# Up projections of a gated feed-forward layer: ten feature tiles by Strassen's seven products, where there were six such tiles

## The chip, the cores and the metric

The kernel runs on one core of a Trainium2 chip. The metric is the device time of one execution in microseconds. All times below come from one profiled execution or from repeated timed runs.

## The reference, cut to what matters

The kernel computes one encoder block: three token mixers, a gated merge with an output projection onto the residual, and a gated feed-forward layer with a convolution over tokens. The change lies in that last layer. S = 512 tokens, D = 1024, D_FF = 2816, all float32.

```python
def rms_norm(x, g):
    return x * lax.rsqrt(jnp.mean(x * x, axis=-1, keepdims=True) + EPS) * g

def conv_glu_ffn(h, w_up, w_conv, b_conv, w_down):
    a, u = jnp.split(h @ w_up, 2, axis=-1)          # w_up: 1024 x 5632
    return (jax.nn.gelu(dwconv3(a, w_conv, b_conv)) * u) @ w_down

x = x + merged @ w_out                               # the output projection
x = x + conv_glu_ffn(rms_norm(x, ffn_norm_g), w_up, w_conv, b_conv, w_down)
return rms_norm(x, final_norm_g)
```

## The kernel before, in words

Everything is held transposed, features on partitions and the 512 tokens along the free axis. Each float32 operand is split in a high half, rounded to the format that TensorE takes at full rate (fp32r), and a low half, the rest. A product is three matmuls, high x high, high x low and low x high (`mm3`, L370 to L372). A weight block comes from memory as a raw tile (`emit_raw`, L246; three raw buffers, `wr`), ScalarE rounds it (L336) and VectorE subtracts (L337); the split weights lie in a ring of four buffers (`w`). A planner, `weights`, emits these steps a fixed number of blocks ahead. Engines take their instructions in the order in which they stand in the program, so the order of emission is the order of each queue. `in_turn` keeps the chained steps of an engine in order; its helper's line is L270.

The output projection's loop (L1312 to L1323) makes eight feature tiles of x2, the new residual. Each is scaled and split (L376, L377) into HH and HL, and its squares are summed on POOL into `acc` (L1323). The row norm of x2 follows: the sum is transposed (L177), written to memory and read back (`td`, `U`), reduced (L202), scaled (L203), raised to -1/2 on POOL (L204), transposed (L205), written and read back broadcast as `rb` (L208, L210). The up projections do not wait for it: the norm's factor is applied to their result, in `conv` (L570: product with rb; L572 to L574: the three taps) and on POOL (L1453, then L270) after the gelu (L1451, with a table load on ScalarE). The product with the other projection is L1467 (VectorE).

The up projections run over 22 feature tiles f. A normal tile has two projections, `ua` and `uu`, of 8 blocks each: 16 products of 128 x 128 x 512. A tile in `SUP` takes both projections together as a 2 x 2 block product by Strassen's scheme with seven products instead of eight, on halves of 256 tokens (`up_seven`; products 1, 2, 4, 5, 7, 3, 6 in that order): in all 7 x 4 products of 128 x 128 x 256,. It needs differences of x's blocks (`x_forms(p)` for four pairs p of feature tiles: three differences on VectorE, L1341 to L1343; their rounding on ScalarE, L1345; two remainders on VectorE, L1346 and L1347) and sums of weight blocks. Product 1's weights are a difference made on VectorE (L1383). Four other products' sums are made by DMA: `up_load` loads one summand into a `ut` tile (SP), `up_sum` adds the other with an accumulating DMA (POOL). `up_weight` rounds and subtracts such weights (L1390 ScalarE, L1391 VectorE). A tile that is not in `SUP` is called a normal tile below: its 16 products of 512 columns are what 8 x 4 of 256 would be.

The down projection takes the first twelve feature tiles in seven products too (blocks "s") and the other ten plainly (blocks "k"), in an order `DOWN` with plain blocks between the others. Its sums are loaded late (L246 on a unit tile `u`, SP) with an accumulating DMA on POOL (L270). The residual x2 is transposed in tiles 3 to 10 (`turn_out`: L177 and four DMAs to memory) and loaded back (`turn_in`, L186) in tiles 6 to 13. The weights of a `SUP` tile come as one block `ub`.

Of the kernel before, what the change touches and what calls it, by code (L numbers as in the profile page):

```python
# [12 lines left out]
F32R = mybir.dt.float32r  # L13
# [4 lines left out]
P = 128  # L18
S = 512
# [6 lines left out]
NSP = 6  # L26
NOK = FT - 2 * NSP
HELD = 4
SUP = (5, 7, 9, 11, 13, 15)
UP_ORDER = (1, 2, 4, 5, 7, 3, 6)  # L30
HC = D // 2
NU = 14
# [105 lines left out]
def hybrid_block(ctx, tc, xT, memT, wflat, vecs, gbias, nabias, out):  # L138
# [121 lines left out]
        q = slice(j * HC, (j + 1) * HC)  # L260
        return lw[0][:, q], lw[1][:, q]

    ur, uf = [], {}

    chain = {}

# [1045 lines left out]
    for f in range(KT):  # L1312
        xr = scr()
        SY.dma_start(xr, xT[:, f, :])
        ps = proj(("out", f), GH, GL)
        V.tensor_tensor(x2[f], ps, xr, op=ALU.add)
        split_act(HH[f], HL[f], x2[f], vcol("ffn_g", f))
        if f == 0:
            A.activation(acc2, x2[f], AF.Square)
        else:  # L1320
            sq = scr()
            A.activation(sq, x2[f], AF.Square)
            G.tensor_tensor(acc2, acc2, sq, op=ALU.add)  # L1323


    x2v = [u[:, :4 * S].rearrange("p (f s) -> p f s", f=4) for u in x2u]
    ur.extend(unit() for _ in range(NSP // 2))
    ou, UH, UL = [], [], []
    res, turns = {}, {}
    xf = [unit(F32R) for _ in range(5)]  # L1330
    XF = (5, 2, 6, 7, 1)
    uw = {}

    def x_forms(p):

        y, d = ur[2][:, p % 2 * D:(p % 2 + 1) * D], ur[1][:, :5 * M]
# [8 lines left out]
        A.activation(h, d, AF.Copy)  # L1345
        V.tensor_tensor(xf[p][:, 5 * M:8 * M], d[:, :3 * M], h[:, :3 * M].bitcast(F32), op=ALU.subtract)  # L1346
        V.tensor_tensor(xf[4][:, p * S:(p + 1) * S], d[:, 3 * M:], h[:, 3 * M:].bitcast(F32), op=ALU.subtract)  # L1347

    def x_of(i, p):
# [27 lines left out]
    def up_weight(f, n):  # L1377
# [13 lines left out]
        V.tensor_tensor(l, src, h.bitcast(F32), op=ALU.subtract)  # L1391
        uw[f, "w", i] = h, l

    def up_seven(f):

        b12, b45, b7, b36 = [atps() for _ in range(4)]
        at = {1: b12[:, :M], 2: b12[:, M:], 4: b45[:, :M], 5: b45[:, M:], 7: b7[:, :M], 3: b36[:, :M], 6: b36[:, M:]}
        ta, tu = scr(), scr()
        t00, t01, t11 = ta[:, :M], tu[:, :M], tu[:, M:]
        for n, i in enumerate(UP_ORDER):  # L1400
            if n + 2 < len(UP_ORDER):
                up_weight(f, n + 2)
            elif n + 2 == len(UP_ORDER):
                emit_split(st["split"])
                st["split"] += 1
            wh, wl = uw.pop((f, "w", i))
            for p in range(KT // 2):
                c = slice(p * P, (p + 1) * P)
                xh, xl = x_of(i, p)
                mm3(at[i], wh[:, c], wl[:, c], xh, xl, p == 0, p == KT // 2 - 1)  # L1410
            if i == 2:
                A.activation(ta, b12, AF.Copy)
                A.activation(t11, at[2], AF.Copy, scale=-1.0)
                V.tensor_tensor(t11, t11, at[1], op=ALU.add)
# [12 lines left out]
    for f in range(FT):  # L1427
        if f == 0:
            wa, wu = weights(("ua", f)), weights(("uu", f))
            pa, pu = mmps(), mmps()  # L1430
            for k in range(KT - 1):
                mm3(pa, wa[k][0], wa[k][1], HH[k], HL[k], k == 0, False)
            for k in range(KT - 1):
                mm3(pu, wu[k][0], wu[k][1], HH[k], HL[k], k == 0, False)
            t2 = turn_in(turn_out(by4(acc2)), "nab", 2)
            k = KT - 1
            mm3(pa, wa[k][0], wa[k][1], HH[k], HL[k], False, True)
            mm3(pu, wu[k][0], wu[k][1], HH[k], HL[k], False, True)
# [9 lines left out]
        if f + 2 in SUP:  # L1448
            up_load(f + 2)
        c = conv(pa, rb2, "ffw", "ffb", f, FT)  # L1450
        A.activation(c, c, AF.Gelu_apprx_tanh)  # L1451
        if "G" not in chain:
            chain["G"] = G.tensor_tensor(c, c, rb2, op=ALU.mult).ins  # L1453
        else:
            in_turn("G", "tensor_tensor", c, c, rb2, op=ALU.mult)
        if f < KT // 2:
            x_forms(f)
        if f > 0 and f not in SUP:
            if f + 1 in SUP:
                ws = weights(("uu", f))  # L1460
                uw[f + 1] = split.pop(BINDEX["ub", f + 1][0])
                for n in range(2):
                    up_weight(f + 1, n)
                split[BINDEX["uu", f][0]] = ws
            pu = pu1 if f == 1 else proj(("uu", f), HH, HL)
        if f < 2 * NSP:
            V.tensor_tensor(ur[f // 4][:, f % 4 * S:(f % 4 + 1) * S], pu, c, op=ALU.mult)  # L1467
# [279 lines left out]
```

## Time and profile before

| | us |
|---|---|
| timed runs: median of three | 851.61 (851.08 to 853.33) |
| the profiled execution | 851.33 |
| its span in the trace | 849.6 |
| TensorE busy | 841.0, 99% |
| VectorE / ScalarE / POOL busy | 622.4 / 476.4 / 175.6 |
| output projection ends, up projections begin | 494.7 |
| up projection of tile 2 begins | 516.5 |
| down projection begins | 731.2 |

The profile's times count from the span's start. A row of a timeline gives start, length, engine, line, operation, out<-in with its shapes, the number of merged instructions, and in brackets the idle time of the engine just before with what ended it. PE is TensorE, DVE VectorE, ACT ScalarE, POOL GpSimd, and SPq or POOLq the DMAs issued by SP or POOL. The lengths of matmuls are pipelined; what a matmul costs is the distance of the starts.

### The profile page before, as it was taken

The numbers are of one execution on the slowest core, as the hardware profiler recorded it, in microseconds if no ns is written. First come the engines' busy times: TensorE is split into PE (matmuls) and PEld (weight loads), VectorE is DVE, ScalarE is ACT, GpSimd is POOL, SyncE is SP. The second block draws the span as 40 slices with busy tenths as digits, with TensorE's granted clock in tenths as the row PEclk, the third lists the DMA queues.
The fourth block names the chain that finished last, engine by engine and source line by source line (L and its number), as shares of the span: only waits on it lengthen the run. The fifth ranks groups of instructions, "written<-read, shape, count | busy, mean of one in ns | idle before, by whom it ended". The sixth has DMA issues, their size and how long they took to land.

```text
span 849.6 us, 12743 instructions
## 1 busy us (share of the span) xinstructions
PE 841.0 (99%) x4214; PEld 716.3 (84%) x4214; DVE 622.4 (73%) x1246; ACT 476.4 (56%) x992; POOL 175.6 (21%) x268
## 2 busy tenths in 40 slices
PE   9999999999999999999999999999999999999997
PEld 8898988888888888888888888799999888888885
DVE  6699777766458748998676666877777856687893
ACT  7465557775446548888644644444455544444562
POOL 2000200000101840454000121423332111320421
PEclk9999999999999999999999999999999999999999
DMA  8236736563425856788743343588886333895882
GB/s 273 84 114 202 246 120 205 168 198 102 145 90 172 229 145 199 223 250 234 232 140 109 117 159 99 132 235 226 224 229 147 101 109 124 234 231 143 250 197 99
DMA packets 86226, 147.32 MB, mean 173 GB/s; under 512 B 11784, under 2 KB 38920, under 8 KB 86160
## 3 DMA queue, kind: packets, MB, share of 16 engines
q1 hardware_dynamic: 71600, 127.47, 46.9%
q0 software_dynamic: 14272, 18.90, 12.2%
q8 instruction: 33, 0.54, 0.3%
q14 instruction: 33, 0.27, 0.1%
q10 hardware_dynamic: 288, 0.14, 0.1%
HBM read 130.84 MB, written 15.62 MB: 172 GB/s over the span
## 4 chain that ended last, share of the span: by engine, by line
PE 91%; DMA 3%; DVE 2%; issue 2%; ACT 1%; POOL 0%; SPq 0%; POOLq 0%; DVEq 0%; ACTq 0%
PE mm L372 23%; PE mm L370 23%; PE mm L371 23%; PE at L372 6%; PE at L371 6%; PE at L370 6%; DMA s<-xT 2%; PE at L1033 1%; PE at L866 1%; PE at L868 1%; PE at L850 1%; DVE w L337 1%; PE at L404 0%; PE at L999 0%; PE at L1000 0%
## 5 line engine op out<-in xcount | busy, mean ns | idle before, releaser
L370 PE MATMUL mm<-u,w 128*128 128x512 f32 x763 | 298.8, 392 | 0.0
L372 PE MATMUL mm<-u,w 128*128 128x512 f32 x763 | 297.5, 390 | 1.0 <-DVE w L337 1.0
L371 PE MATMUL mm<-u,w 128*128 128x512 f32 x763 | 297.5, 390 | 0.0
L337 DVE TENSOR_TENSOR w<-wr,w 128x512 fp32r<-128x512 f32 (+2 forms) x233 | 159.8, 690 | 69.9 <-ACT w L336 68.5
L336 ACT ACTIVATE w<-wr 128x512 fp32r<-128x512 f32 (+2 forms) x232 | 144.8, 627 | 113.0 <-PE mm L372 72.2
L372 PEld LDWEIGHTS mm<-u,w 128*128 128x128 f32 x763 | 143.4, 188 | 32.0 <-DVE w L337 1.8
L371 PEld LDWEIGHTS mm<-u,w 128*128 128x128 f32 x763 | 143.5, 188 | 28.6
L370 PEld LDWEIGHTS mm<-u,w 128*128 128x128 f32 x763 | 143.5, 188 | 28.5
L679 POOL DMA_DIRECT2D u<-nav_d x128 | 62.3, 505 | 99.8 <-PE at L1033 52.3
L270 POOL TENSOR_TENSOR s<-s,rb 128x512 f32<-128x512 f32 x21 | 31.1, 1480 | 154.4 <-ACT s L1451 151.0
L372 PE MATMUL at<-u,w 128*128 128x256 f32 (+1 forms) x200 | 60.2, 301 | 0.0
L371 PE MATMUL at<-u,w 128*128 128x256 f32 (+1 forms) x200 | 60.0, 300 | 0.0
L370 PE MATMUL at<-u,w 128*128 128x256 f32 (+1 forms) x200 | 60.0, 300 | 0.0
L270 ACT ACTIVATE w<-u 128x512 fp32r<-128x512 f32 x52 | 32.7, 632 | 41.5 <-PE mm L372 20.6
L370 PE MATMUL mm<-w,u 128*128 128x512 f32 x128 | 50.4, 394 | 0.0
L372 PE MATMUL mm<-w,u 128*128 128x512 f32 x128 | 49.9, 390 | 0.0
L371 PE MATMUL mm<-w,u 128*128 128x512 f32 x128 | 49.9, 390 | 0.0
L270 DVE TENSOR_TENSOR w<-u,w 128x512 fp32r<-128x512 f32 x52 | 35.7, 688 | 18.1 <-ACT w L270 17.5
L572 ACT ACTIVATE s<-pad,vec 128x512 f32<-128x512 f32 x30 | 24.3, 812 | 27.6 <-DVE pad L570 24.3
L371 PEld LDWEIGHTS at<-u,w 128*128 128x128 f32 x200 | 38.2, 191 | 1.5
L370 PEld LDWEIGHTS at<-u,w 128*128 128x128 f32 x200 | 38.2, 191 | 1.5
L372 PEld LDWEIGHTS at<-u,w 128*128 128x128 f32 x200 | 38.2, 191 | 1.3
(333 smaller groups left out, 1390.3 us busy)
## 6 DMA issues: line engine op xcount, KB each, us to landing
wr<-wflat SPq DMA_DIRECT2D x118, 512.0 KB, 3.7
u<-wflat SPq DMA_DIRECT2D x50, 256.0 KB, 5.7
td<-s SPq DMA_DIRECT2D x172, 64.0 KB, 1.9
U<-td SPq DMA_DIRECT2D x41, 256.0 KB, 4.0
s<-xT SPq DMA_DIRECT2D x24, 256.0 KB, 4.0
ut<-wflat SPq DMA_DIRECT2D x24, 256.0 KB, 4.3
ut<-wflat POOLq DMA_DIRECT2D x24, 256.0 KB, 7.3
u<-wflat POOLq DMA_DIRECT2D x24, 256.0 KB, 7.6
```

The lines of the kernel that those rows point to most:

```text
L270: chain[eng] = getattr({"V": V, "A": A, "G": G}[eng], what)(*a, **k).ins
L336: A.activation(h[:, u:v], src, AF.Copy)
L337: V.tensor_tensor(l[:, u:v], src, h[:, u:v].bitcast(F32), op=ALU.subtract)
L370: PE.matmul(ps, lh, rh, start=start, stop=False)
L371: PE.matmul(ps, lh, rl, start=False, stop=False)
L372: st["mm"] = PE.matmul(ps, ll, rh, start=False, stop=stop).ins
L572: A.activation(t1, pad[:, 0:512], AF.Identity, scale=vcol(w, i), bias=vcol(b, i))
L679: G.dma_start(vw[r * 32:(r + 1) * 32, i * 256:(i + 1) * 256], nav_v[hf, r, CW[b]:CW[b] + 32, hp * 256:(hp + 1) * 256])
L850: PE.matmul(pv[:, i, 0:129], kt[:, d, i], va[:, i + d, h, 0:129], start=True, stop=True)
L866: PE.matmul(pv[:, d, 0:129], E[J // 2][:, 2 * (J % 2) + d, :], va[:, J, h, 0:129], start=True, stop=not inter)
L868: PE.matmul(pv[:, d, 0:129], Q[d][:, i, :], C[:, d, i, 0:129], start=False, stop=True)
L1033: PE.matmul(py[:, bl * 256:(bl + 1) * 256], vw[:, c:c + P], pp[bl][:, hf * 256:(hf + 1) * 256], start=hf == 0, stop=hf == 1)
```

## The change

- `SUP` has ten tiles, 2, 4, ... 20, in place of six, 5, 7, ... 15. Each of the ten makes its four `ut` loads and accumulating DMAs.
- `x_forms(0)` moves into the output projection's loop, after its fourth tile; pairs 1, 2, 3 follow in tile 0's code: 1 behind the loads of the norm's sum (`turn_in(turn_out(...))`), 2 and 3 behind the call of `rstd_row_turned`. They were called in tiles 0 to 3, each behind its tile's gelu.
- Tile 2's weights: `up_load` at the start of tile 0, `up_sum` behind the norm's transpose, and the first two splits (`up_first`) behind tile 1's `uu`.
- `up_seven` takes two banks of each PSUM ring in place of four of one.
- The turned residual is loaded back in the last tile, eight DMAs of 256 KB into two units (L1499), in place of one in each of tiles 6 to 13. The high and low halves of tiles 12 to 15 lie in the buffers that the residual had ("H" and "R").

```diff
-SUP = (5, 7, 9, 11, 13, 15)
+SUP = (2, 4, 6, 8, 10, 12, 14, 16, 18, 20)
...
     for f in range(KT):
         xr = scr()
...
             A.activation(sq, x2[f], AF.Square)
-            G.tensor_tensor(acc2, acc2, sq, op=ALU.add)
+            chain["G"] = G.tensor_tensor(acc2, acc2, sq, op=ALU.add).ins
+        if f == 3:
+            x_forms(0)
...
+    def up_first(f):
+
+        uw[f] = split.pop(BINDEX["ub", f][0])
+        for n in range(2):
+            up_weight(f, n)
+
     def up_seven(f):
 
-        b12, b45, b7, b36 = [atps() for _ in range(4)]
+        b12, b45, b7, b36 = atps(), atps(), mmps(), mmps()
...
         if f == 0:
+            up_load(SUP[0])
...
             t2 = turn_in(turn_out(by4(acc2)), "nab", 2)
+            up_sum(SUP[0])
+            x_forms(1)
...
             rb2 = rstd_row_turned(t2, "2")
+            x_forms(2)
+            x_forms(3)
             pu1 = proj(("uu", 1), HH, HL, bank=atps)
+            up_first(SUP[0])
         elif f in SUP:
             pa, pu = up_seven(f)
         else:
-            if f + 1 in SUP:
+            if f + 1 in SUP[1:]:
                 up_sum(f + 1)
...
-        if f < KT // 2:
-            x_forms(f)
...
-            if f % 2 == 0:
-                ou.append(unit(F32R))
-            for i, part in enumerate((UH, UL)):
-                a = f % 2 * 2 + i
-                part.append(ou[-1][:, a * S:(a + 1) * S])
+            if f < 2 * NSP + 4:
+                for tag, part in zip("HR", (UH, UL)):
+                    part.append(tp.tile([P, S], F32R, tag=tag, name=nm("UH"), bufs=4))
+            else:
+                if f % 2 == 0:
+                    ou.append(unit(F32R))
+                for i, part in enumerate((UH, UL)):
+                    a = f % 2 * 2 + i
+                    part.append(ou[-1][:, a * S:(a + 1) * S])
             split_act(UH[-1], UL[-1], c)
...
-        if 6 <= f < 14:
-            t, g = (f - 6) % NT, (f - 6) // NT
-            res[t, g] = turn_in(turns[t, g], "HR"[g], 4)
+        if f == FT - 1:
+            for g in (1, 0):
+                u = unit()
+                for t in range(NT):
+                    q = u[:, t * S:(t + 1) * S]
+                    SY.dma_start(q, turns[t, g])
+                    res[t, g] = q.rearrange("p (i s a) -> p s i a", i=4, a=32)
```

In the changed kernel's file the lines move: L1326 to L1328 are x's differences, L1330 their rounding, L1331 and L1332 the remainders, L1338 the residual's addition, L1389 product 1's difference, L1396 and L1397 the split of seven-product weights, L1478 the product with the gelu; L570 to L574, L202 to L210 and L337 stay.

VectorE before, from the norm's reduction to the first two tiles' products with the gelu (`U`, `y`: the norm; `w` and `wr`: split and raw weights; `pad`: conv's input):

```order
L202 TENSOR_REDUCE y_5451<-U_5410 128x4
L337 TENSOR_TENSOR w_5423<-wr_5343,w_5423 128x512
L203 TENSOR_SCALAR y_5451<-y_5451 128x4
L205 STREAM_TRANSPOSE y_5453<-y_5452 128x32
L337 TENSOR_TENSOR w_5468<-wr_5351,w_5468 128x512
L337 TENSOR_TENSOR w_5471<-wr_5351,w_5471 128x512
L337 TENSOR_TENSOR w_5533<-wr_5418,w_5533 128x512
L570 TENSOR_TENSOR pad_150<-mm_5359,rb_5464 128x512
L570 TENSOR_TENSOR pad_153<-at_5426,rb_5464 128x512
L337 TENSOR_TENSOR w_5536<-wr_5418,w_5536 128x512
L573 SCALAR_TENSOR_TENSOR s_5500<-pad_150,vec,s_5500 128x512
L573 SCALAR_TENSOR_TENSOR s_5516<-pad_153,vec,s_5516 128x512
```

The same place after, in two pieces: first from x's last differences to the norm's last transpose, then from the first conv on (`u` of L1326 to L1332: x's differences; `ut`: a weight sum made by DMA):

```order
L1326 TENSOR_TENSOR u_5009<-u_5010 128x512
L337 TENSOR_TENSOR w_5369<-wr_5308,w_5369 128x512
L1327 TENSOR_TENSOR u_5009<-u_5010 128x512
L1328 TENSOR_TENSOR u_5009<-u_5010 128x256
L337 TENSOR_TENSOR w_5446<-wr_5356,w_5446 128x512
L202 TENSOR_REDUCE y_5477<-U_5423 128x4
L1331 TENSOR_TENSOR u_5501<-u_5009,u_5501 128x768
L337 TENSOR_TENSOR w_5449<-wr_5356,w_5449 128x512
L203 TENSOR_SCALAR y_5477<-y_5477 128x4
```

```order
L570 TENSOR_TENSOR pad_153<-at_5452,rb_5490 128x512
L1397 TENSOR_TENSOR w_5582<-wr_5364,w_5582 128x512
L573 SCALAR_TENSOR_TENSOR s_5546<-pad_150,vec,s_5546 128x512
L573 SCALAR_TENSOR_TENSOR s_5554<-pad_153,vec,s_5554 128x512
L574 SCALAR_TENSOR_TENSOR s_5546<-pad_150,vec,s_5546 128x512
L574 SCALAR_TENSOR_TENSOR s_5554<-pad_153,vec,s_5554 128x512
L1426 TENSOR_TENSOR s_5566<-s_5566,at_5561 128x256
L1397 TENSOR_TENSOR w_5600<-ut_5350,w_5600 128x512
L1397 TENSOR_TENSOR w_5615<-ut_5352,w_5615 128x512
L1478 TENSOR_TENSOR u_5347<-mm_5373,s_5546 128x512
L1478 TENSOR_TENSOR u_5347<-at_5512,s_5554 128x512
L1430 TENSOR_TENSOR s_5565<-s_5565,at_5562 128x512
```

x's differences now stand ahead of the norm's reduction and between it and L203, and the low halves of tile 2's later products (w_5582 is product 5's, w_5600 7's, w_5615 3's; 6's follows) stand behind the first conv and its products.

SP's queue in tile 21 after: the last sums and raw weights of the down projection with the eight loads of the turned residual (`td`) among them:

```order
L246 DMA wr_7846<-wflat 128x512
L246 DMA u_7742<-wflat 128x512 x3
L1499 DMA u_7830<-td_6245 128x512
L1499 DMA u_7830<-td_6388 128x512
L1499 DMA u_7830<-td_6477 128x512
L1499 DMA u_7830<-td_6620 128x512
L1499 DMA u_7835<-td_5781 128x512
L1499 DMA u_7835<-td_5924 128x512
L1499 DMA u_7835<-td_6013 128x512
L1499 DMA u_7835<-td_6156 128x512
L246 DMA u_7742<-wflat 128x512
L246 DMA wr_7861<-wflat 128x512
```

Before, there were no such loads here; wr_7861, the raw weights of the down projection's first plain block, now stands behind the eight of them.

More of the change, by code (lines that the diff above doesn't have):

```diff
@@ L261, in lastw @@
         return lw[0][:, q], lw[1][:, q]
-    ur, uf = [], {}
+    uf = {}
     chain = {}
@@ L1311, in hybrid_block @@
     acc2 = cp.tile([P, S], F32, name="acc_2", tag="acc", bufs=1)
[L1312 to L1330, printed above, removed]
     XF = (5, 2, 6, 7, 1)
-    uw = {}
+    uw, xf = {}, {}
+    ur = [None] + [unit() for _ in range(2)]
     def x_forms(p):
+        for q in (p, 4):
+            if q not in xf:
+                xf[q] = unit(F32R)
         y, d = ur[2][:, p % 2 * D:(p % 2 + 1) * D], ur[1][:, :5 * M]
@@ L1347, in x_forms @@
         V.tensor_tensor(xf[4][:, p * S:(p + 1) * S], d[:, 3 * M:], h[:, 3 * M:].bitcast(F32), op=ALU.subtract)
+    for f in range(KT):
+        xr = scr()
+        SY.dma_start(xr, xT[:, f, :])
+        ps = proj(("out", f), GH, GL)
+        V.tensor_tensor(x2[f], ps, xr, op=ALU.add)
+        split_act(HH[f], HL[f], x2[f], vcol("ffn_g", f))
+        if f == 0:
+            A.activation(acc2, x2[f], AF.Square)
+        else:
+            sq = scr()
+            A.activation(sq, x2[f], AF.Square)
+            chain["G"] = G.tensor_tensor(acc2, acc2, sq, op=ALU.add).ins
+        if f == 3:
+            x_forms(0)
+    x2v = [u[:, :4 * S].rearrange("p (f s) -> p f s", f=4) for u in x2u]
+    ur[0] = unit()
+    ur.extend(unit() for _ in range(NSP // 2 - 3))
+    ou, UH, UL = [], [], []
+    res, turns = {}, {}
     def x_of(i, p):
@@ L1444, in hybrid_block @@
         else:
-            if f + 1 in SUP:
+            if f + 1 in SUP[1:]:
                 up_sum(f + 1)
             pa = pa1 if f == 1 else proj(("ua", f), HH, HL)
-        if f + 2 in SUP:
+        if f + 2 in SUP[1:]:
             up_load(f + 2)
@@ L1451, in hybrid_block @@
         A.activation(c, c, AF.Gelu_apprx_tanh)
[L1452 to L1455, printed above, removed]
-        if f < KT // 2:
-            x_forms(f)
+        in_turn("G", "tensor_tensor", c, c, rb2, op=ALU.mult)
         if f > 0 and f not in SUP:
-            if f + 1 in SUP:
+            if f + 1 in SUP[1:]:
                 ws = weights(("uu", f))
-                uw[f + 1] = split.pop(BINDEX["ub", f + 1][0])
-                for n in range(2):
-                    up_weight(f + 1, n)
+                up_first(f + 1)
                 split[BINDEX["uu", f][0]] = ws
@@ L1469, in hybrid_block @@
             V.tensor_tensor(c, pu, c, op=ALU.mult)
[L1470 to L1474 removed]
+            if f < 2 * NSP + 4:
+                for tag, part in zip("HR", (UH, UL)):
+                    part.append(tp.tile([P, S], F32R, tag=tag, name=nm("UH"), bufs=4))
+            else:
+                if f % 2 == 0:
[3 more added lines that the diff above has]
+                    part.append(ou[-1][:, a * S:(a + 1) * S])
             split_act(UH[-1], UL[-1], c)
```

## The prediction

> **What bounds the kernel now.** I read the busy times first, then a table of stretches, then what TensorE waits for.
>
> ```profile
> PE 841.0 (99%) x4214; PEld 716.3 (84%) x4214; DVE 622.4 (73%) x1246; ACT 476.4 (56%) x992; POOL 175.6 (21%) x268
> ...
> 489.00:516.00 27.00, 27.00 (x120) 22.35 (x120) 14.68 (x23) 10.70 (x18) 4.69 (x4) 1.00 0.52 168
> 516.00:530.00 14.00, 14.00 (x63) 11.60 (x62) 10.37 (x16) 8.55 (x12) 2.72 (x2) 1.00 0.19 56
> 530.00:553.00 23.00, 21.95 (x105) 17.89 (x104) 19.40 (x33) 11.19 (x17) 10.23 (x7) 1.00 0.56 133
> 553.00:616.00 63.00, 63.00 (x398) 57.32 (x397) 49.05 (x83) 30.22 (x55) 18.36 (x18) 1.00 0.87 227
> ...
> PE mm L372 <- DVE w L337: 1.0, 1, 1.0
> ```
>
> The first row is the page's. The four stretches give the length, the busy time of PE, PEld, DVE, ACT and POOL, the granted clock, the DMA share and GB/s. The last row is the only wait of TensorE from the output projection (489) to the end. TensorE is busy 841.0 of 849.6 us at a full clock, so only two things move the time: fewer TensorE cycles, or a wait where there was none. In 553 to 616, where normal and seven-product tiles already alternate, TensorE loses nothing, at 0.87 of the DMA engines and 49 of 63 us of VectorE. So a seven-product tile in the middle is covered, and I cost its added DMAs and additions at nothing there: they lie beside the 10.9 us of the normal tile ahead, and a sum that landed 1 us late would cost 1 us in each pair. The edges are what has to be worked out: the first such tile, and the way into the down projection.
>
> **Four more seven-product tiles.** A normal tile has 48 matmuls of 512 columns (two projections, 8 blocks, three each); a seven-product tile has 84 of 256 (7 products, 4 blocks, three each).
>
> ```profile
> 505.60 0.39 PE L370 MATMUL at<-u,w 128*128 128x512 f32 x1
> ...
> 516.48 0.39 PE L370 MATMUL mm<-u,w 128*128 128x512 f32 x1
> ...
> 560.84 0.40 PE L370 MATMUL mm<-u,w 128*128 128x512 f32 x1
> ...
> 602.86 0.40 PE L370 MATMUL mm<-u,w 128*128 128x512 f32 x1
> ```
>
> Tile 1 runs from the first row to the second: 10.88 us, 0.227 a matmul (0.39 is the pipelined length, not the pitch). The last two rows are the starts of tiles 6 and 10, two pairs apart: 42.02 / 2 = 21.01 a pair, so the seven-product tile takes 10.13, or 0.1206 a matmul. It saves 0.75, and four more save **3.0 us**. [...]
>
> **The wait at tile 4.** TensorE was busy 21.95 of 23.00 us in 530 to 553: **-1.05**. It stood at the second weights of a normal tile 4, behind VectorE's x differences of pairs 2 and 3. Tile 4 is now a seven-product tile and those differences are done earlier. If another instruction takes that place, the gain is 0; I take it whole, since the cause moves.
>
> **Tile 2, the dear one.** The change puts the differences of pairs 1 to 3 on VectorE and ScalarE between 494 and 516, ahead of and between the steps of the row norm (rb). Before, the tile-2 weights were split ahead of all that hangs on rb. Now five of the seven are split behind the first conv.
>
> ```profile
> 501.12 0.71 DVE L177 STREAM_TRANSPOSE s<-acc 128x512 f32<-128x512 f32 x1 [1.21 <-POOL acc L1323]
> ...
> 507.86 0.69 DVE L202 TENSOR_REDUCE y<-U 128x4 f32<-128x512 f32 x1 [1.39 <-DMA U<-td]
> 509.07 0.16 DVE L203 TENSOR_SCALAR y<-y 128x4 f32<-128x4 f32 x1
> ...
> 518.46 0.69 DVE L570 TENSOR_TENSOR pad<-mm,rb 128x512 f32<-128x512 f32 x1 [3.15 <-DMA rb<-rd]
> 519.07 0.68 DVE L570 TENSOR_TENSOR pad<-at,rb 128x512 f32<-128x512 f32 x1
> 520.27 1.41 DVE L573 SCALAR_TENSOR_TENSOR s<-pad,vec,s 128x512 f32<-128x512 f32 x2
> 521.60 1.40 DVE L574 SCALAR_TENSOR_TENSOR s<-pad,vec,s 128x512 f32<-128x512 f32 x2
> ...
> 519.24 1.52 ACT L572 ACTIVATE s<-pad,vec 128x512 f32<-128x512 f32 x2 [1.93 <-DVE pad L570]
> 521.30 1.28 ACT L1451 ACT_TABLE_LOAD   x1
> 522.59 1.15 ACT L1451 ACTIVATE s<-s 128x512 f32<-128x512 f32 x2
> 524.96 1.26 ACT L1345 ACTIVATE u<-u 128x1280 fp32r<-128x1280 f32 x1
> ...
> 509.31 1.04 POOL L204 TENSOR_TENSOR y<-y,nhalf 128x4 f32<-128x4 f32 x1 [8.22 <-DVE y L203]
> ...
> 523.30 1.47 POOL L1453 TENSOR_TENSOR s<-s,rb 128x512 f32<-128x512 f32 x1 [12.96 <-DMA wr<-wflat]
> 524.73 1.30 POOL L270 TENSOR_TENSOR s<-s,rb 128x512 f32<-128x512 f32 x1
> 526.06 0.69 DVE L1467 TENSOR_TENSOR u<-at,s 128x512 f32<-128x512 f32 x1 [0.57 <-POOL s L270]
> 527.33 0.95 DVE L1346 TENSOR_TENSOR u<-u,u 128x768 fp32r<-128x768 f32 x1
> 528.20 0.68 DVE L1347 TENSOR_TENSOR u<-u,u 128x512 fp32r<-128x512 f32 x1
> ```
>
> These are VectorE, ScalarE and POOL around rb in the kernel before. Back to back a 512-column instruction of VectorE takes 0.60 (519.07 - 518.46), a multiply-add 0.66 (two in 1.33), one of 768 columns 0.87 (528.20 - 527.33).
>
> *rb itself.* The transpose of the squares' sum is some 0.5 late, behind a remainder of pair 1 (501.6); after it come 0.65 of its own, a split (0.60) and pair 2's last differences (0.33). So pair 2's rounding on ScalarE (1.26) starts at 503.2 and ends at 504.5. Behind it VectorE has pair 2's two remainders (0.87 + 0.60), pair 3's differences (0.60, 0.60, 0.33), and two weight splits (1.20): 508.75. Then come the reduction (0.60), pair 3's 768-column remainder, which waits for ScalarE's second rounding (508.2 to 509.5; 0.87 more, 510.4), one more split (0.60) and only then L203: 511.1 where it was 509.07. Power, transpose and two DMAs follow as before, so rb lands near **520.5**, 2.05 later. Before, VectorE idled 3.15 us for rb and TensorE didn't notice. The bounds: 0 (if the two ran side by side) and 3.5 (all of pair 3's five instructions, 3.0, and a split beside them, counted in full).
>
> *What then waits.* Tile 2 begins at 516.48 with a pitch of 0.1206.
> - Product 5 needs its low half at its third matmul: 516.48 + 38 x 0.1206 = 521.06. VectorE does two convs' L570 and then that split: 520.5 + 0.61 + 0.60 + 0.68 = 522.4. Wait 1.3.
> - Product 7's low half, due 12 matmuls on (523.85), stands behind four multiply-adds (2.7), one addition of 256 columns (0.33) and itself (0.68): 526.1. Wait 2.25.
> - Product 6's low half stands behind both tiles' products with the gelu. ScalarE after rb: two L572 to 522.8, then two weight roundings and two copies (some 2.0) to 524.8, the table load to 526.1; 0.71 to POOL (523.30 - 522.59), two POOL multiplies of 1.43 and 1.33 to 529.55; VectorE: the product 0.61, an addition 0.60, the split 0.68: 531.4. TensorE would be there at 526.1 + 24 x 0.1206 + 3 x 0.227 (three of tile 3's matmuls stand before it) = 529.7, and 0.3 later by the rounding for one of those three. Waits 0.3 and 1.4.
>
> Sum **+5.3** (531.4 against 516.48 + 74 x 0.1206 + 0.68 = 526.1). With rb on time it would still be 5.3 - 2.05 = 3.25, the lower end; with the 3.5 above it is 6.7. None of it is hidden: TensorE has no slack. Two edits here cost nothing: products 7 and 3/6 now take PSUM banks of the other ring, which the first gelu product (529.55 - 1.33 + 0.61 = 528.8) frees before tile 3's bank is asked for (529.0); the first four held tiles' halves lie in the buffers that the turned residual had.
>
> **Tile 4's sums.** Its accumulating POOL DMAs stand behind a product with the gelu that is late now.
>
> ```profile
> 565.72 3.59 POOL L270 DMA_DIRECT2D ut<-wflat  x4
> ut<-wflat POOLq DMA_DIRECT2D x24, 256.0 KB, 7.3
> ```
>
> Four issues of 0.9 us and 7.3 to landing cost nothing in the running pairs. For the first pair I take **+0.3** between 0 and 2 (two issues), near the pairs. The four of tile 2 itself are issued ahead of POOL's power (L204), where POOL idled 8.22 us.
>
> **The end.** Eight loads of the turned residual (256 KB each), before spread over tiles 6 to 13, now stand together in SP's queue in tile 21, behind three loads for the sums of the down projection and ahead of the raw weights of its fifth block (the first plain one).
>
> ```profile
> 731.22 0.39 PE L370 MATMUL at<-w,uf 128*128 128x512 f32 x1
> ...
> 724.69 3.05 SPq L246 DMA_DIRECT2D wr<-wflat  x2
> ...
> 730.50 27.47 SPq L246 DMA_DIRECT2D u<-wflat  x18
> ...
> 703.00:705.00 2.00, 2.00 (x11) 1.65 (x10) 0.75 (x2) 0.69 (x2) 0.00 (x0) 1.00 1.00 367
> ...
> 730.00:770.00 40.00, 40.00 (x179) 33.12 (x178) 28.43 (x46) 19.69 (x33) 11.85 (x13) 1.00 0.96 236
> ...
> ACT w L270 <- DMA u<-wflat: 3.7, 3, 2.0
> ...
> wr<-wflat SPq DMA_DIRECT2D x9, 256.0 KB, 4.3
> ```
>
> The down projection starts at 731.22 (before's time); its fifth block is due after four blocks of 6 matmuls, 24 x 0.227 = 5.44, so at 736.7, and its split (0.65) must start at 736.0. The raw load was issued at 724.69 or just after. Now 12 loads go first, from about 725.1: at 367 GB/s a load takes 0.71 us, and with its own it lands at 725.1 + 13 x 0.71 = 734.4, in time; at the 236 GB/s of this stage a load takes 1.11, and it lands at 739.5, 3.5 late. From the landing of the last of the 12 loads at the faster rate, 733.6, and the median landing of 4.3 it is 737.9. I take **+1.4**, between 0 and 3.5, since ScalarE waits here even now (up to 2.0 for one load, by the row) with TensorE untouched: some microseconds of slack exist, but few. The loads for the sums behind it start some 5 us later and their accumulating DMAs with them; between 0 and the longest wait of ScalarE for such a load today (2.0) may come on top. I take **+0.5**, nearer 0, since a late block puts off the next ones' due times too.
>
> **Sum.** -3.0 - 1.05 + 5.3 + 0.3 + 1.4 + 0.5 = +3.45, on the profiled execution's 851.33 (span 849.6 and 1.73 around it; 0.28 under the median 851.61): **854.8 us**.
>
> **Rivals.** Some 0.3% (2.55 us) is what a measurement can tell: faster is under 849.06, slower over 854.16.
> - *Tile 2 waits, the end hides its loads* (or tile 2 waits only 3.25): -4.05 + 5.3 + 0.3 = +1.55, 852.9; with 3.25 and no other wait 850.5. For it: at 734.4 the block is in time. Against: a DMA share of 0.96. Chance 0.25, no difference.
> - *Tile 2 doesn't wait* (the other side): rb's chain and the splits keep ahead of TensorE, and the gain of 4.05 is whole: 847.3. It decides where rb lands before 515.2 (5.3 earlier than 520.5); for it speaks that VectorE is busy in only 14.68 of the 27.00 us from 489 to 516, against it that rb came at 518.46 even with that room. Chance 0.15.
> - *The end starves*: block after block of the down projection is late, 3.5 for the fifth and 2 to 3 more for the sums: 854.8 + 4 = 858.8. For it: 0.96 and 236 GB/s; against: no TensorE wait there now. Chance 0.11.
> - [...] Chance 0.01.
>
> The forecast's own case has 0.48, with 853 to 857 as its range; a fifth of it is within 0.3%. So slower 0.48 x 0.8 + 0.12 = 0.50, the same 0.25 + 0.10 = 0.35, faster 0.15. From 850.0 to 858.5 the range leaves out the gain case and half of the starved one.
>
> **What would show it.** Right: waits of TensorE on VectorE's split of the seven-product weights (L1397), three of 1 to 2.3 us between 521 and 532; L570 near 520.5; tiles 4 to 20 in pairs of 21.0; one wait near the down projection's fifth block. Wrong: rb at 518.5, no wait in tile 2, or loads at the end with TensorE full through 731 to 790.

## Result: slower by 1.0%, 860.5 us, where 854.8 was predicted

The changed kernel takes 860.51 us (median of four runs, 859.03 to 862.09) against 851.60 before: a ratio of 1.0101, 95% interval 1.0077 to 1.0126. The direction was right, the size was not: +8.9 us, not +3.2, and outside the range (858.5). The profiled execution took 859.75, its span is 858.0. First the busy times and TensorE's waits from the output projection on, then the stretches of the prediction's table, all of the changed kernel:

```profile
PE 843.2 (98%) x4358; PEld 723.7 (84%) x4358; DVE 641.6 (75%) x1286; ACT 485.0 (57%) x1016; POOL 188.8 (22%) x284
...
PE at L372 <- DVE w L1397: 2.8, 2, 2.6
PE mm L370 <- ACT w L270: 1.9, 1, 1.9
PE mm L372 <- DVE w L1397: 1.5, 1, 1.5
PE at L372 <- DVE w L337: 0.8, 1, 0.8
...
516.00:530.00 14.00, 9.90 (x65) 9.09 (x64) 8.06 (x14) 6.84 (x12) 1.64 (x2) 0.86 0.38 122
530.00:553.00 23.00, 22.98 (x136) 20.62 (x136) 18.63 (x31) 11.28 (x20) 7.78 (x8) 0.94 0.63 156
553.00:616.00 63.00, 62.78 (x392) 56.67 (x391) 49.01 (x84) 30.03 (x54) 19.18 (x18) 1.00 0.81 201
731.00:790.00 59.00, 57.08 (x245) 46.40 (x244) 43.47 (x69) 27.50 (x46) 11.63 (x13) 0.97 0.97 289
```

Most of the waits are where they were forecast: on the splits of tile 2 (L1397; 0.2 of the 2.8 us is in tile 6) and on ScalarE's rounding of the down projection's fifth block. The 0.8 us in tile 1 (L337) were not. That the sum, 7.0 us, is near the forecast's 7.5 is chance. In the rows of the stretches, the granted clock has something new: 0.86 and 0.94 in the first two stretches and 0.97 in the down projection. And waits are not losses; those are read from the starts of TensorE's rows:

| stretch, from the starts in the timeline | before | after | lost (+) or gained |
|---|---|---|---|
| start of tile 2 | 516.48 | 517.62 | +1.1 |
| tiles 2 and 3, against a running pair's 20.98 | | 28.17 | +7.2 |
| tiles 4 to 21, against nine running pairs (188.8) | | 189.83 | +1.0 |
| what ten such pairs (209.8) save over 516.48 to 731.22 before | 214.74 | | -4.9 |
| down projection's start to the last matmul | 111.69 | 115.62 | +3.9 |

The sum is 8.3 of the 8.4 us between the spans.

**Tile 2.** Here are VectorE, SP and POOL around the norm's factor rb after the change:

```profile
500.12 3.56 POOL L270 DMA_DIRECT2D ut<-wflat  x4
...
500.95 2.07 SPq L180 DMA_DIRECT2D td<-s  x4
510.27 0.34 SPq L186 DMA_DIRECT2D U<-td  x1
...
506.79 0.68 DVE L337 TENSOR_TENSOR w<-wr,w 128x512 fp32r<-128x512 f32 x1
513.01 0.69 DVE L202 TENSOR_REDUCE y<-U 128x4 f32<-128x512 f32 x1 [5.54 <-DMA U<-td]
515.08 0.16 DVE L203 TENSOR_SCALAR y<-y 128x4 f32<-128x4 f32 x1
522.98 0.69 DVE L570 TENSOR_TENSOR pad<-mm,rb 128x512 f32<-128x512 f32 x1 [4.22 <-DMA rb<-rd]
524.19 0.68 DVE L1397 TENSOR_TENSOR w<-wr,w 128x512 fp32r<-128x512 f32 x1
527.77 1.28 DVE L1397 TENSOR_TENSOR w<-ut,w 128x512 fp32r<-128x512 f32 x2
532.88 0.68 DVE L1397 TENSOR_TENSOR w<-ut,w 128x512 fp32r<-128x512 f32 x1
```

And the DMA queues from 500 to 511 (packets, MB, share of the 16 DMA engines; the 1.05 MB of q0 are POOL's four sums of 256 KB, q1 is what SP issued):

```profile
q0 software_dynamic: 576, 1.05, 61.3%
q1 hardware_dynamic: 588, 0.28, 10.5%
```

VectorE was not what made rb late: it stood ready at 507.4 and idled 5.54 us. The four small transposing DMAs (`td`), issued at 500.95, had landed only at 510.27, when SP could issue the read back: 9.3 us, where it was 3.3 before (501.86 to 505.15, the profile before). Beside them POOL had issued tile 2's four accumulating DMAs at 500.12, and these took most of the DMA engines' time. While VectorE stood there, a split of tile 1's weights behind the reduction (L337) was late too, and TensorE waited 0.8 us for it: most of the 1.1 us ahead of tile 2. So rb came at 522.98, not 520.5, and the three splits behind it (524.2, 527.8, 532.9) as late as the steps of the prediction make them from there.

**The clock.** TensorE's rows through the two waits:

```profile
522.05 0.28 PE L371 MATMUL at<-u,w 128*128 128x256 f32 x1
524.92 0.39 PE L372 MATMUL at<-u,w 128*128 128x256 f32 x1 [2.59 <-DVE w L1397]
...
526.14 0.42 PE L372 MATMUL at<-u,w 128*128 128x256 f32 x1
526.36 0.41 PE L370 MATMUL mm<-u,w 128*128 128x256 f32 x1
528.50 0.58 PE L372 MATMUL mm<-u,w 128*128 128x256 f32 x1 [1.52 <-DVE w L1397]
...
532.73 0.35 PE L370 MATMUL mm<-u,w 128*128 128x256 f32 x1
532.91 0.28 PE L371 MATMUL mm<-u,w 128*128 128x256 f32 x1
```

One us after the first wait the pitch goes from 0.120 to 0.213 us, with TensorE busy, and it comes back at 532.8, some 6.9 us later. There is the temptation to book some 23 slow matmuls x 0.093 = 2.1 us as the price (1.5 of the 6.9 us are the second wait). It is less: product 6's low half came at 533.56, and at full speed TensorE would have stood at about 532.1 and waited for it. The matmul that needs it started at 534.37, where one that waits starts 0.05 behind its split (524.87 to 524.92), so the half clock can have cost 0.8 us at most here. Experiments 4, 5 and 9 measure it.

**The end.** SP, ScalarE and TensorE at the down projection's fifth block:

```profile
731.74 4.49 SPq L1499 DMA_DIRECT2D u<-td  x8
737.24 0.33 SPq L246 DMA_DIRECT2D wr<-wflat  x1
...
742.46 0.63 ACT L270 ACTIVATE w<-wr 128x512 fp32r<-128x512 f32 x1 [2.55 <-DMA wr<-wflat]
746.29 0.63 ACT L270 ACTIVATE w<-wr 128x512 fp32r<-128x512 f32 x1 [2.68 <-DMA wr<-wflat]
...
740.84 0.39 PE L372 MATMUL at<-w,uf 128*128 128x512 f32 x1
743.14 1.19 PE L370 MATMUL mm<-w,UH 128*128 128x512 f32 x4 [1.92 <-ACT w L270]
744.75 0.63 PE L371 MATMUL mm<-w,UH 128*128 128x512 f32 x1
748.13 0.40 PE L372 MATMUL at<-w,uf 128*128 128x512 f32 x1
```

The raw weights were issued behind the eight loads, at 737.24, and landed at 742.4; TensorE stood for 2.1 us (740.84 + 0.23 to 743.14) and some 1.5 us later its matmuls took 0.63 in place of 0.39 (a pitch of 0.43, not 0.227) until about 748. By the starts the standing and the slow stretch (1.7 us) make up the loss of 3.9; TensorE has no other wait there.

### The profile page after: what moved, and what is told of

It reads as the page before. It is cut to its first block, busy times and chain, and to the rows that moved or that the text cites. A ratio compares the mean times of both kernels' runs of the same rounds, so it can differ in the third digit from the quotient of the medians.

```text
span 858.0 us, 13170 instructions
## 1 busy us (share of the span) xinstructions
PE 843.2 (98%) x4358; PEld 723.7 (84%) x4358; DVE 641.6 (75%) x1286; ACT 485.0 (57%) x1016; POOL 188.8 (22%) x284
## 4 chain that ended last, share of the span: by engine, by line
PE 89%; DMA 4%; issue 3%; DVE 1%; POOL 1%; SPq 0%; ACT 0%; POOLq 0%; DVEq 0%; ACTq 0%
PE mm L372 23%; PE mm L370 23%; PE mm L371 23%; PE at L372 5%; PE at L371 5%; PE at L370 5%; DMA ut<-wflat 1%; PE at L1033 1%; DMA td<-s 1%; PE at L866 1%; PE at L868 1%; PE at L850 1%; DMA wr<-wflat 1%; DMA u<-td 1%; PE at L404 0%
## 5 line engine op out<-in xcount | busy, mean ns | idle before, releaser
L370 PE MATMUL mm<-u,w 128*128 128x512 f32 (+1 forms) x819 | 308.9, 377 | 0.0
L372 PE MATMUL mm<-u,w 128*128 128x512 f32 (+1 forms) x819 | 307.2, 375 | 1.5 <-DVE w L1397 1.5
L371 PE MATMUL mm<-u,w 128*128 128x512 f32 (+1 forms) x819 | 307.4, 375 | 0.0
L337 DVE TENSOR_TENSOR w<-wr,w 128x512 fp32r<-128x512 f32 (+2 forms) x217 | 147.3, 684 | 57.5 <-ACT w L336 55.6
L336 ACT ACTIVATE w<-wr 128x512 fp32r<-128x512 f32 (+2 forms) x216 | 134.8, 627 | 84.8 <-PE mm L372 60.8
L372 PEld LDWEIGHTS mm<-u,w 128*128 128x128 f32 x819 | 155.2, 190 | 29.6 <-DVE w L1397 1.8
L370 PEld LDWEIGHTS mm<-u,w 128*128 128x128 f32 x819 | 155.6, 190 | 26.2 <-ACT w L336 0.5
L371 PEld LDWEIGHTS mm<-u,w 128*128 128x128 f32 x819 | 155.5, 190 | 25.8
L372 PE MATMUL at<-u,w 128*128 128x256 f32 (+1 forms) x192 | 58.5, 305 | 3.7 <-DVE w L1397 2.8
L371 PE MATMUL at<-u,w 128*128 128x256 f32 (+1 forms) x192 | 57.8, 301 | 0.0
L370 PE MATMUL at<-u,w 128*128 128x256 f32 (+1 forms) x192 | 57.7, 301 | 0.0
L372 PEld LDWEIGHTS at<-u,w 128*128 128x128 f32 x192 | 36.7, 191 | 6.0 <-DVE w L1397 3.4
L371 PEld LDWEIGHTS at<-u,w 128*128 128x128 f32 x192 | 36.6, 191 | 1.7
L370 PEld LDWEIGHTS at<-u,w 128*128 128x128 f32 x192 | 36.6, 191 | 1.6
L370 PE MATMUL mm<-w,u 128*128 128x512 f32 x96 | 37.8, 394 | 0.0
L372 PE MATMUL mm<-w,u 128*128 128x512 f32 x96 | 37.4, 390 | 0.0
L371 PE MATMUL mm<-w,u 128*128 128x512 f32 x96 | 37.4, 389 | 0.0
```

Of the source, the lines that this page charges most:

```text
L336: A.activation(h[:, u:v], src, AF.Copy)
L337: V.tensor_tensor(l[:, u:v], src, h[:, u:v].bitcast(F32), op=ALU.subtract)
L370: PE.matmul(ps, lh, rh, start=start, stop=False)
L371: PE.matmul(ps, lh, rl, start=False, stop=False)
L372: st["mm"] = PE.matmul(ps, ll, rh, start=False, stop=stop).ins
```

## The experiments

Ratios are to the kernel before, timed on the same chip. "Pair" is the distance of the starts of two seven-product tiles; "end" is the time from the down projection's first matmul to the last one (111.7 before, 115.6 after). One profile goes with each.

**1. Tile 2's sums in the output projection.**

```diff
         if f == 3:
             x_forms(0)
+            up_load(SUP[0])
+        if f == 5:
+            up_sum(SUP[0])
...
-            up_sum(SUP[0])
             x_forms(1)
```

> The changed kernel, with tile 2's four accumulating DMAs (and their loads) issued in the output projection's sixth tile, some 15 us ahead of the norm's transpose, not beside it. Theory A (the norm's small transposing DMAs were held up by the four 256 KB sums on the same DMA engines): they land in about 3 us again as in the kernel before, not 9; the reduction is then bound by VectorE's own queue at about 508, rb lands near 518 in place of 523.0, and tile 2's waits shrink from 8.3 us to some 3: about 5 us faster than the changed kernel, 855 us. Rival (VectorE's added differences are what makes rb late): rb stays at 521 or later, and the time within 1.5 us of 860.5.

858.1 us (ratio to before 1.0071, 1.0056 to 1.0085): 2.4 less than the changed kernel, half of what was expected. The transposing DMAs landed in 3.3 us again (504.45 to 507.73), but they had started 3.5 later. POOL and VectorE of this kernel (L1356 is the residual's addition):

```profile
487.77 3.55 POOL L270 DMA_DIRECT2D ut<-wflat  x4
...
499.54 0.69 DVE L1356 TENSOR_TENSOR u<-mm,s 128x512 f32<-128x512 f32 x1 [3.64 <-DMA s<-xT]
...
s<-xT SPq DMA_DIRECT2D x3, 256.0 KB, 7.7
```

Now the row of x for the eighth tile stood beside the sums, took 7.7 us (the row's median of three loads; 4.0 for the 24 loads of the kernel before) and held VectorE for 3.64. rb came at 521.1. The sums delayed what was in flight beside them in both kernels (9.3 us in place of 3.3 there, 7.7 against 4.0 here); the first theory holds as to the cause, and the edit only moved the victim.

**2. The turned residual behind the first raw weights.**

```diff
-                    SY.dma_start(q, turns[t, g])
...
     for n, key in enumerate(DOWN):
         wh, wl = weights(key)
+        for t, g in RES_AT.get(n, ()):      # n = 2: four, n = 6: two, n = 10: two
+            SY.dma_start(...)               # turned residual (t, g)
```

> The changed kernel, with the eight loads of the turned residual issued in the down projection, four behind its third block, two behind the seventh and two behind the eleventh, so that the raw weights of the fifth block go ahead of them; the same bytes. Theory (order in SP's queue): no wait at the fifth block (1.92 before), no half clock there; 2 to 4 us faster, 856.5 to 858.5. Rival (the bytes themselves, 2 MB in a stage that keeps the DMA engines full): the wait moves to a later block, and the time stays at 860 or rises.

857.81 us (1.0067, 1.0053 to 1.0081), 2.7 less (1.6 between the profiled spans). The wait at the fifth block is gone, with the half clock behind it; the end took 113.8. Three waits of 0.2 and a total of 2.1 us remain against 111.7. So both had a part here: SP's order some 1.8 us, the 2 MB in a stage whose DMA engines are full (a share of 1.02 from 736 to 756 and 1.00 from there to 776) 2.1. In experiment 9 the same order left 0.7; why it differs is open.

**3. The first convs behind tile 2's splits.**

```diff
-        c = conv(pa, rb2, "ffw", "ffb", f, FT)
...
+            def later(f=f, pa=pa, pu=pu):    # called in up_seven(2): tile 0's behind the fifth split, tile 1's behind the sixth
+                with tc.issue_after(st["low"]):
+                    c = conv(pa, rb2, "ffw", "ffb", f, FT)
+                ...
```

> The changed kernel, with the first two tiles' convs, gelus and products put behind the weight splits of tile 2's first five products on VectorE; the sums stay where they are, so rb is as late (523). Theory (in order behind rb on VectorE is what makes the splits late): no wait at products 5 and 7, one of about 2 us at product 3, whose split now stands behind the first conv: 4 to 5 us faster, about 856. Rival (the splits are late since their sums or buffers are late): waits as before, 860.

861.74 us (1.0114, 1.0098 to 1.0131): no faster, though what the edit aims at happened. Tiles 2 and 3 took 25.1 us in place of 28.2, with waits under 0.9 and no half clock, at an rb as late as before (523.4). But the next pairs took 24.6 and 22.9 in place of 21.1 and 21.5. POOL, VectorE and TensorE here:

```profile
542.17 3.58 POOL L270 DMA_DIRECT2D ut<-wflat  x4
...
543.52 0.69 DVE L1397 TENSOR_TENSOR w<-s,w 128x512 fp32r<-128x512 f32 x1
...
544.26 0.39 PE L372 MATMUL at<-u,w 128*128 128x256 f32 x1 [1.41 <-DVE w L1397]
```

Tile 4 starts at 545.8 in the changed kernel and at 542.5 here, but what it needs comes no earlier. Product 1's low half is split at 543.5 (543.8 in the changed kernel), behind the late multiply-adds and gelu product on VectorE: 1.6 us. Tile 4's sums are issued at 542.2 (542.05 there), behind tile 2's gelu product, and the later splits wait for them: some 1.9 us. So the 3.1 us won in tile 2 are lost again. The wait was a cover for the next ones.

**4. TensorE kept busy through tile 2's waits.**

```diff
+            if f == SUP[0] and i in (5, 7):
+                for _ in range(22 if i == 5 else 12):
+                    PE.matmul(at[i], wh[:, :P], x_of(i, 0)[0], start=True, stop=True)
             for p in range(KT // 2):
```

> The changed kernel with 22 more matmuls of 256 columns ahead of product 5 of tile 2 and 12 ahead of product 7, whose results are overwritten: TensorE stays busy through the two waits. Both theories: the clock stays at 1.00 from 526 to 533. Theory A (what comes next is bound by data that is late anyway): the half clock cost under 1 us net there, 859.5 to 860.5. Rival B (the half clock costs what it takes, 32 matmuls at 0.213 in place of 0.120): 3 us faster, 857.5.

In tile 2 it did what it was made for; the stretch behind the waits, in the changed kernel and then here:

```profile
526.00:533.00 7.00, 5.48 (x27) 5.19 (x26) 5.07 (x10) 5.45 (x10) 2.54 (x2) 0.51 0.43 148
```

```profile
527.00:534.00 7.00, 5.56 (x45) 5.15 (x43) 5.04 (x9) 5.72 (x11) 2.57 (x2) 1.00 0.47 152
...
PE mm L372 <- DVE w L1397: 1.9, 2, 1.4
```

The clock stayed at 1.00 and 45 matmuls ran in place of 27. But then TensorE stood before product 6, 1.4 us, a wait that the half clock had covered, and tiles 2 and 3 took 27.77 in place of 28.17: 0.4 us for a half clock of 6.9. That is rather too little: in the changed kernel three of tile 3's matmuls (0.7 us) stand ahead of that wait, and here behind it. As a whole the kernel was slower, 863.75 us (1.0139, 1.0113 to 1.0164), for its wait at the fifth block was 5.7 us and later pairs took 21.3 to 22.0. Why these grew with an edit in tile 2 alone is open.

**5. Tile 2's sums one by one.**

```diff
+    up_load(SUP[0])
     for f in range(KT):
...
+        if f in (0, 1, 2, 3):
+            up_sum(SUP[0], sums[(0, 1, 2, 3).index(f)])
```

> The changed kernel, with tile 2's four sums issued one by one in the output projection's first four tiles. In e1 they stood together in the sixth tile and the row of x for the eighth took 7.7 us to land, so the delay had only moved from one small transfer to another. Theory (four sums at once hold the DMA engines for some 6 us, whoever is beside them): apart from each other, and 20 us before the norm, they delay nothing; rb lands at 518 to 519, tile 2 and 3 take 23.5 to 25 us (28.2 in the changed kernel, 26.0 in e1), 856 to 857 us. Rival (rb is bound by VectorE's differences of x): rb stays at 521 as in e1, and the time at 858.

856.29 us (1.0051, 1.0039 to 1.0063), as expected. rb came at 519.5, and tiles 2 and 3 took 24.94.

```profile
502.13 0.71 DVE L177 STREAM_TRANSPOSE s<-acc 128x512 f32<-128x512 f32 x1 [1.18 <-POOL acc L1365]
509.32 0.68 DVE L202 TENSOR_REDUCE y<-U 128x4 f32<-128x512 f32 x1
519.50 0.69 DVE L570 TENSOR_TENSOR pad<-mm,rb 128x512 f32<-128x512 f32 x1 [3.92 <-DMA rb<-rd]
```

The reduction (L202) no longer waits for the DMA but starts back to back behind VectorE's own work, as the prediction had it. Tile 2 starts without a wait ahead of it, at 516.74. So the four sums beside the norm's transpose cost 3.2 of the 7.2 us in tiles 2 and 3 and 0.9 of the 1.1 ahead of them; the other 4.0 stand behind rb all the same.

**6. Nine tiles from tile 3**, 3, 5, ... 19, the sums as in 5, the turned residual in tile 20.

```diff
-SUP = (2, 4, 6, 8, 10, 12, 14, 16, 18, 20)
+SUP = (3, 5, 7, 9, 11, 13, 15, 17, 19)
...
-        if f == FT - 1:
+        if f == 20:
             for g in (1, 0):
```

> Nine seven-product tiles, 3, 5, ... 19; sums of the first one by one as in e5, so tile 2 is a normal tile whose weights are split before rb; x's pieces are free one tile earlier, and the turned residual is loaded in tile 20. Theory (the saving of 0.8 a tile is real; only the start and the end gave it back): three tiles save 2.4 and the wait at tile 4 goes, 1.05; one wait of about 1 us at tile 3: 849 to 850 us, faster than both kernels. Rival (sums and differences cost TensorE something wherever they are): no faster than 852.

850.59 us, ratio 0.9981 (0.9972 to 0.999): faster than both, if only by 0.2% of the kernel before. The end is 111.7 again. Three pairs took 21.7, with waits of 0.4 to 0.5 in each, for sums that landed late, as experiment 10 shows.

**7. Nine tiles from tile 4**, 4, 6, ... 20, x's differences of pairs 1 to 3 in tiles 1 to 3, the end as in the changed kernel.

> Nine seven-product tiles, 4, 6, ... 20: the changed kernel without tile 2 and with x's differences of pairs 1 to 3 in tiles 1 to 3 as before; the end as in the changed kernel. Theory: nothing waits in tile 2; the wait at tile 4 may stay (1 to 2 us, since the differences of pair 3 end at 542 and tile 4 starts at 538); the end costs its 3.9 us: -2.4 + 1 + 3.9, 853 to 855 us. Rival (the end's cost comes from the lateness of tile 2): no wait at the fifth block, 850.

855.28 us (1.0041, 1.0028 to 1.0054). Nothing waits in tile 2 (rb at 517.8); tile 4 waits 0.8 and 1.1 us, for ScalarE's rounding of its weights, and a half clock follows from 542.6 to 545.8. The fifth block waits 2.0 us and the end takes 115.6, as in the changed kernel: its loss does not hang on tile 2.

**8. Waits in steps in the kernel before**, to see whether a wait alone is enough for the half clock. The additions idle and change no result.

```diff
+SLOW = {16: 9, 18: 11, 20: 13}
...
+                for _ in range(SLOW.get(key[1], 0) if key[0] == "ua" and a == 0 else 0):
+                    in_turn("D", "tensor_tensor", slow, h[:, u:v].bitcast(F32), h[:, u:v].bitcast(F32), op=ALU.add)
...
                 V.tensor_tensor(l[:, u:v], src, h[:, u:v].bitcast(F32), op=ALU.subtract)
```

> The kernel before, with 9, 11 and 13 idle additions of 0.6 us on VectorE ahead of one low half in tiles 16, 18 and 20, where TensorE has no wait and a clock of 1.00. Waits of about 1, 2 and 3 us are wanted. [...] Rival (the half clock in the changed kernel had another cause, such as the load on the DMA engines): clock 1.00 throughout.

The waits came out as 3.55, 0.58 and 1.01, and 3.92 us (other work of VectorE mixed in). Here is TensorE at the first, and then the stretches behind the first, around the middle two, and behind the last; L378 to L380 are the three matmuls:

```profile
668.42 0.40 PE L379 MATMUL mm<-u,w 128*128 128x512 f32 x1
672.37 0.50 PE L380 MATMUL mm<-u,w 128*128 128x512 f32 x1 [3.55 <-DVE w L345]
...
673.30:680.00 6.70, 6.05 (x15) 4.26 (x14) 4.14 (x7) 1.69 (x3) 1.29 (x1) 0.50 0.49 157
700.00:712.00 12.00, 10.41 (x44) 7.93 (x44) 7.70 (x14) 3.86 (x6) 0.00 (x0) 1.00 0.39 131
726.50:731.00 4.50, 4.50 (x12) 3.45 (x12) 3.73 (x7) 0.25 (x1) 0.00 (x0) 0.50 0.32 111
```

A wait alone, of 3.55 and of 3.92 us, in a place with no rb, no seven products and half-idle DMA engines (a share of 0.49 and 0.32 in the two slow rows), halved the clock to 0.50. The waits of 0.58 and 1.01, 3 us apart, didn't: 1.00.

**9. Experiments 2 and 5 together.**

> The changed kernel with e2 and e5 together: tile 2's sums spread over the output projection, the turned residual's loads in the down projection. Theory (the two losses are separate): 4.2 and 2.7 us off 860.5, so 853 to 854.5, and what is left over the kernel before is tile 2's splits behind rb (some 4 us) and 2 us in the down projection, against a saving of 4. Rival (the second loss is a consequence of the first): no better than 856.

853.15 us (1.0012, 1.0003 to 1.0022), as expected: the two losses add up. The end took 112.4. This run and 5 have the same wait of 1.9 us in tile 2, and the half clock follows it in one of them only. Here, then in 5:

```profile
520.00:525.00 5.00, 3.00 (x23) 2.60 (x22) 5.00 (x9) 4.97 (x9) 0.00 (x0) 1.00 0.43 105
525.00:528.00 3.00, 3.00 (x18) 3.00 (x17) 1.07 (x3) 2.44 (x6) 2.54 (x2) 0.56 0.54 172
```

```profile
520.00:525.00 5.00, 3.14 (x25) 2.75 (x23) 5.00 (x10) 4.68 (x8) 0.00 (x0) 1.00 0.29 105
525.00:528.00 3.00, 2.98 (x24) 2.98 (x25) 1.26 (x2) 2.93 (x7) 2.38 (x2) 1.00 0.50 160
```

Tiles 2 and 3 took 25.28 with it and 24.94 without. In the down projection 5 waited 2.2 us at the fifth block without a half clock, and its end took 115.4; the changed kernel's, with one, 115.6. But 5 stood 0.3 us longer at that block, and its next block waited twice more (0.4 and 0.2), where the changed kernel, at half clock, did not. From the fifth block's first matmul to the sixteenth it is 4.69 us in 5 (739.40 to 744.09) and 5.22 in the changed kernel (743.14 to 748.36). So the half clock cost 0.3 us in tile 2 here and 0.5 at the end.

**10. Experiment 6 with later sums ahead of the gelu product on POOL.**

```diff
         if f + 2 in SUP[1:]:
             up_load(f + 2)
+            up_sum(f + 2)
         c = conv(pa, rb2, "ffw", "ffb", f, FT)
...
-            if f + 1 in SUP[1:]:
-                up_sum(f + 1)
```

> e6 with the sums of each later seven-product tile issued on POOL ahead of the preceding seven-product tile's gelu product, not behind it. In e6 the sums of tiles 9, 11 and 13 are issued at the start of those tiles' predecessors' second half and three waits of 0.5 us and pairs of 21.7 us are left there. Theory (those sums land late): issued some 5 us earlier, pairs of 21.0 again, 1.5 to 2 us faster than e6, 848.5 to 849. Rival (loads and transposes fill the DMA engines there): as e6, 850.6, or slower since POOL now waits for the loads ahead of the product.

847.29 us, ratio 0.9951 (0.9936 to 0.9966): the best version, better than expected. TensorE has no wait from the output projection to the end, and every pair is 20.98.

```profile
490.00:560.00 70.00, 70.00 (x389) 61.40 (x388) 54.99 (x89) 38.10 (x60) 18.45 (x15) 1.00 0.58 160
560.00:731.00 171.00, 171.00 (x1032) 153.59 (x1031) 137.56 (x225) 89.04 (x153) 49.33 (x45) 1.00 0.67 181
731.00:790.00 59.00, 59.00 (x262) 48.87 (x261) 45.30 (x73) 27.80 (x45) 9.56 (x11) 1.00 0.91 263
```

**11. Experiment 9 with the convs behind tile 2's splits (3) and the sums first (10).**

> e9 with two edits more: the first two convs, gelus and products behind tile 2's first five splits on VectorE (as e3), and later sums issued ahead of the gelu product (as e10). Theory (what is left in tile 2 is splits that stand behind rb): tiles 2 and 3 take 21 to 22.5 us in place of 25.3, later pairs 21.0, and the time is 848.5 to 850. Rival (VectorE has too much work there in any order): tiles 2 to 5 lose as much together as in e9, 852 or more.

851.04 us (0.999, 0.9981 to 0.9999). Tiles 2 and 3 take 22.53 in place of 25.28, so most of what was left there was the order behind rb; but tile 4 takes 11.51, 1.3 more than in 9, with a wait of 1.2 us for a split, so that half of the gain is lost again. The end takes 113.8 with the residual's loads in it; these two put the time 1 us over what was expected. The down projection starts at 729.9 here and at 727.5 in experiment 10: ten tiles starting at 2 are worth less than nine starting at 3. The end adds the rest of the distance.

## Why the prediction was wrong, step by step

- **Four more tiles** (-3.0) **and the wait at tile 4** (-1.05): right, somewhat too small: together -4.9. A running pair takes 20.98 and a seven-product tile 10.07. The wait stood in tile 3, not in tile 4 (531.74; tile 3 began at 516.48 + 10.88 = 527.4), still behind VectorE's differences of x, and had cost 1.6 us (tiles 2 to 4 took 34.28 before, 32.65 without it).
- **rb** is the step that failed. It was put at 520.5, 2.05 late, by VectorE's added work; it came at 522.98, 4.5 late, and for another reason. The prediction noted that the four sums "are issued ahead of POOL's power (L204), where POOL idled 8.22 us" and looked at POOL's queue alone. What counted was the DMA engines that they share with the norm's transposing DMAs: 9.3 us in place of 3.3. The transpose itself, put 0.5 late, came 0.9 early (500.21). VectorE's part, with the sums away, is 1.0 and not 2.05 (experiment 5). Its rule for what then waits is right as a rule: 10.9 us from rb to product 6's split were forecast, and 522.98 to 533.56 is 10.6. With rb at 519.5 (experiment 5) tiles 2 and 3 lose 24.94 - 20.98 = 4.0 where its working gives 5.3 - 1.0 = 4.3.
- **Tile 2**: +5.3 forecast, +8.3 measured from 516.48 (1.1 and 7.2). 4.1 of it are the sums beside the transpose (3.2 and 0.9, experiment 5); of the other 4.2 the order behind rb is 2.7 (11 against 9, with 1.3 of it moved into tile 4), and the rest wasn't taken apart.
- **Tile 4's sums**: +0.3 forecast, 1.0 measured over tiles 4 to 21, in pairs of 21.1 to 21.5. Experiment 10 shows that order on POOL is the reason: with the sums ahead of the gelu product all pairs are 20.98.
- **The end**: +1.9 forecast, +3.9 measured. The wait at the fifth block, 1.92 where 1.4 was taken, is right in place and near in size, with some luck: the eight loads left SP 3.9 us ahead of the down projection (731.74 to 735.62), where 6.1 was assumed. The second part, +0.5, was mis-sized: 1.7 us of slow matmuls followed the wait, and without them later blocks were late (experiment 5). The loads cost 2.1, 2.1 and 0.7 us with a better order in that stage (experiments 2, 11 and 9) and nothing in tile 20 (6, 10).
- **The half clock** is missing from the prediction altogether. It offers itself as the cause, since on paper it is about what was missing: 2.1 at tile 2 and 1.7 at the end, 3.8 of 4.9. The experiments were against it: at tile 2 it cost 0.4 us or a little more (4; 0.8 at most by the changed kernel's own rows) and 0.3 (9 against 5), and at the end 0.5 (9), since it mostly covered waits that would have come anyway.
- **The rivals**: none was it. "The end starves" (858.8) had the right sign, and the end did lose 2.0 us more than forecast, but the larger part of the excess, 3.0 us, stood at tile 2. The 0.01 among the chances is for seven-product tiles that lose time by their 256-column matmuls; no run shows that: seven-product tiles without a wait, four in the changed kernel and all nine in experiment 10, take 10.07 us (84 matmuls at 0.120) where a normal one takes 10.91 (48 at 0.227).

## What to carry to other kernels

A DMA queue that is free is not a free DMA: SP's four `td` transfers took 9.3 us in place of 3.3 beside POOL's four sums. So before a large or accumulating transfer is moved, look which small transfers are in flight beside its new place and who waits for them, and spread it where nobody does. A transfer that must come late in a queue is best put where the stage has engines to spare, since reordering it inside a full stage gave back only a part (1.8 of the 3.9 us in experiment 2, and all of it in tile 20, experiment 6). And when a wait is removed, ask first what it was covering: here late splits and sums of the next seven-product tile were hidden by the wait before them (experiment 3), and a wait by the half clock (experiment 4).

## What was not expected of the hardware

- A wait of TensorE can be followed by a stretch at half pitch (0.43 in place of 0.227 us at 512 columns, 0.213 in place of 0.120 at 256; granted clock 0.50), seen for 3.2 to 6.9 us and beginning with the wait's end or up to 1.5 us later. Five waits of 2.6 us and more were all followed by one (2.59 in the changed kernel, 2.77 in experiment 3, 5.72 in 4, 3.55 and 3.92 in 8), and so were three of five of 1.9 to 2.2 us (1.92 in the changed kernel, 2.04 in 7 and 1.88 in 9 were, 1.88 and 2.22 in 5 weren't). No single wait of up to 1.41 us was (the changed kernel and 3, 4, 5, 8 and 11 have such waits, of 0.8 to 1.41), but two of 0.81 and 1.06 us close together were in 7. What decides it near 2 us, and when the slow stretch begins and ends, these runs don't show.
- Four accumulating DMAs of 256 KB made four transfers of 64 KB beside them take 9.3 us in place of 3.3, and a load of 256 KB beside four others 7.7 (experiment 1) where the median of its kind was 4.0 in the kernel before.
